# Moving the second half's key norm from a free-running thread to written places in the first half's chunk recursion

## The chip, the cores and the metric

The kernel runs on one core of one Trainium2 chip. The metric is the device time of one execution in microseconds (us); smaller is better. Five engines work side by side, each through its own list of instructions: TensorE (PE in the profile; its weight loads are shown apart as PEld), VectorE (DVE), ScalarE (ACT), GpSimd (POOL) and SyncE (SP, which here issues the weight transfers). An instruction that needs another engine's result waits for a semaphore, and what stands behind it in the same list waits with it.

## What is computed

The reference is one layer of a hybrid encoder for 256 tokens of width 2048: two attention branches, one RWKV-7 branch, a gated mix, and an MLP. The change touches only the RWKV-7 branch, 16 heads of 64 channels. Cut to what matters:

```python
kk_raw = k * k_k
r_h, k_h, v_h, a_h, kk = map(per_head, (r, k, v, a, kk_raw))
kk = kk / jnp.maximum(jnp.sqrt(jnp.sum(kk * kk, axis=-1, keepdims=True)), 1e-12)   # the key norm
decay = jnp.exp(-jnp.exp(per_head(w_log)))

def frame(state, inp):
    r_t, w_t, k_t, v_t, kk_t, kka_t = inp
    sa = jnp.einsum('bhvk,bhk->bhv', state, kk_t)
    state = state * w_t[:, :, None, :] - sa[..., None] * kka_t[:, :, None, :] + v_t[..., None] * k_t[:, :, None, :]
    return state, jnp.einsum('bhvk,bhk->bhv', state, r_t)
```

The state is carried over 256 tokens; afterwards every head is normalised (the gate norm of the kernel) and multiplied by a gate.

## The kernel before, in words

**The background work.** Nearly all of the time is a stream of weight blocks of 128x1024 floats. Each is loaded by SP into `raw` (3 buffers), split into a high part `whi` by ACT (L152) and a low part `wlo` by DVE (L153), and multiplied on PE in full 128x512 float matmuls (`gemm`, L168 to L176, and `tok`, L198 and L214).

**The foreground work.** The attention branches and the RWKV branch are Python generators ("threads"). The written program advances a modelled clock by 0.227 us for each large matmul (`tick`); whenever the clock passes a thread's due time the thread emits its next piece, so its small matmuls are written in between the large ones. `yield 2.0` means "come back 2 us later", `yield "kn1"` means "come back once that is marked".

**Who sets the order.** PE's list stands exactly as it is written (`tc.manual_schedule` for PE). The lists of ACT and DVE are arranged by a list scheduler at build time, except for instructions wrapped in `pin` (`tc.keep_in_program_order`), which stay in the order in which they are written. DVE, ACT and PE meet through tiles; a tile of a tag with one buffer can be written again only after the last reader of the one before.

**The RWKV branch.** The 16 heads are done as two halves of four channel tiles (`rwkv_half(0)`, `rwkv_half(1)`). Each half needs its key norm first (`key_norm`): ACT squares four tiles (L635), splits them (L646 on ACT, L647 on DVE), PE sums them per head with the matrix `bones` (L653), DVE clamps the sums (L655), ACT takes Ln and Exp (L659, L662) for a first inverse root, and DVE refines it by a Newton step (L667 to L672). The result is used in `rwkv_half` at L739.

A half ends in a recursion over four chunks of 64 tokens (`for c in range(4)`, L865 on). I call the chunks c0 to c3. In each chunk:

- PE multiplies the state into `xy` (L869, not in c0), ACT and DVE copy it to `rh` (L873, L874);
- PE solves the chunk (L882, mixed with L842, the part of the next chunk that is known already);
- the result goes from PSUM to `XT` in four copies: ACT, DVE for the first half of the heads (L886, L887), then ACT, DVE for the second half. I call them A0, V0, A1, V1;
- PE takes `XT` for the new state and the output (L894, L898, L903), DVE updates the state `PB` (L912 to L915), ACT copies the output (L917).

Between these steps PE works on the background stream. After c3 the half starts `gate_norm`, whose first steps are two groups of squares and splits on ACT and DVE (L944, L947, L948) and four summing matmuls on PE (L954). In the kernel before, the second half's key norm is started as a thread of its own in c0 of the first half (L905, L906), and its pieces come when their due times do. Its tiles: `b` (its squares and inverse roots), `sqh` (high and low part, in the one buffer of the tag `Ti`), `sq` (clamped sums).

Of the kernel before, what the change touches and what calls it, by code (L numbers as in the profile page):

```python
# [10 lines left out]
F32 = mybir.dt.float32  # L11
F32R = mybir.dt.float32r
AF = mybir.ActivationFunctionType
ALU = mybir.AluOpType
# [3 lines left out]
T = 256  # L18
# [32 lines left out]
def hybrid_block(ctx, tc, xt, x, gains, params, consts, lora, gup, wst, out):  # L51
    nc = tc.nc
    V, A, G, PE = nc.vector, nc.scalar, nc.gpsimd, nc.tensor
# [11 lines left out]
    def nm(s):  # L65
        uid[0] += 1
        return f"{s}_{uid[0]}"
# [4 lines left out]
    def mps():  # L72
        return pm.tile([128, 512], F32, tag="mps", name=nm("mps"), bufs=4)
# [25 lines left out]
    def mark(key, value=True):  # L99
        done[key], at[key] = value, clock[0]  # L100

    def start(gen):

        threads.append({"gen": gen, "need": None, "due": clock[0]})
# [146 lines left out]
    rp = p1.enter_context(tc.tile_pool(name="rp", bufs=1))  # L251
# [152 lines left out]
    for h in range(8):  # L404
        ps = qb[h] if h < 3 else unit(upk)
# [187 lines left out]
    bones = rp.tile([128, 128], F32R, name="bones")  # L593
# [34 lines left out]

    def key_norm(hf):
        PR = range(4 * hf, 4 * hf + 4)  # L630
        B6 = rp.tile([128, 6, T], F32, tag="b6", name=nm("b6"), bufs=1)
        rin = [B6[:, i, :] for i in range(4)]
        for i, p in enumerate(PR):
            yield f"k{p}"
            A.activation(rin[i], done[f"k{p}"], AF.Square, scale=P("kk", p))  # L635
        sq = []
        for both in ((0, 1),) if hf == 0 else ((0,), (1,)):
            sqh = []
            for i2 in both:
                s = B6[:, 2 * i2:2 * i2 + 2, :]  # L640
                if hf == 0:
                    hl = [rp.tile([128, 2, T], F32R, tag="BK", name=nm("sqh"), bufs=8) for _ in range(2)]
                else:
                    t = rp.tile([128, 4, T], F32R, tag="Ti", name=nm("sqh"), bufs=1)
                    hl = [t[:, 0:2], t[:, 2:4]]
                A.activation(hl[0], s, AF.Copy)  # L646
                V.tensor_tensor(hl[1], s, hl[0].bitcast(F32), ALU.subtract)  # L647
                sqh.append(hl)
            yield 3.8
            for hl in sqh:  # L650
                ps = mps()
                for n, part in enumerate(hl):
                    PE.matmul(ps.rearrange("p (a b) -> p a b", a=2), bones, part, start=n == 0, stop=n == 1)  # L653
                sq.append(rp.tile([128, 2, T], F32, tag="At", name=nm("sq"), bufs=2))
                V.tensor_scalar(sq[-1], ps.rearrange("p (a b) -> p a b", a=2), 1e-24, None, ALU.max)  # L655
        if hf:
            yield 2.0
        for i2 in range(2):
            A.activation(B6[:, 2 * i2:2 * i2 + 2, :], sq[i2], AF.Ln, scale=float(2.0 ** 20))  # L659
        for i2 in range(2):  # L660
            ri = B6[:, 2 * i2:2 * i2 + 2, :]
            A.activation(ri, ri, AF.Exp, scale=-0.5)  # L662
        yield 4.5
        sc = B6[:, 4:6, :]
        for i2 in range(2):
            ri = B6[:, 2 * i2:2 * i2 + 2, :]
            V.tensor_scalar(ri, ri, 1024.0, None, ALU.mult)  # L667
            V.tensor_tensor(sc, ri, ri, ALU.mult)
            yield 2.0
            V.tensor_tensor(sc, sc, sq[i2], ALU.mult)  # L670
            V.tensor_scalar(sc, sc, -0.5, 1.5, ALU.mult, ALU.add)
            V.tensor_tensor(ri, ri, sc, ALU.mult)  # L672
            yield 3.0
        kin[hf] = rin
        mark(f"kn{hf}")

    def rwkv_half(hf):
        PR = range(4 * hf, 4 * hf + 4)
        xw, xa, wl = done["low"]
        kn, lor = {}, {}  # L680
        kx = {p: done[f"k{p}"] for p in PR} if hf else {}

        def lora_load(p):
            if p in PR:
                lor[p] = rp.tile([128, 2, 128], F32, tag="zx", name=nm("lor"), bufs=1)
# [4 lines left out]
        def lora_split(p):  # L690
            if p in PR:
                raw = lor[p]
# [3 lines left out]

        lora_load(PR[0])
        if hf:
# [10 lines left out]
        rin = kin[hf]  # L709
        SC = rp.tile([128, 32, 128], F32, tag="SC", name=nm("SC"), bufs=1)  # L710
        At, Bt, Kt, bon = {}, {}, {}, {}
        ecol = rp.tile([128, 4, 4], F32, tag="ecol", name=nm("ecol"), bufs=2)
        for i, p in enumerate(PR):
            ps = mps()
# [6 lines left out]
            c = rp.tile([128, T], F32, tag="kkr", name=nm("cs"), bufs=1)  # L721
# [67 lines left out]
        for i2 in range(2):  # L789
            for cc in range(4):  # L790
                for h, hc in enumerate(HC):
                    for i, p in enumerate(PR[2 * i2:2 * i2 + 2]):
                        PE.matmul(pss[h][HC[i], i2 * 256 + cc * 64:i2 * 256 + cc * 64 + 64],
                                  done[f"v{p}"][hc, cc * 64:cc * 64 + 64], C("cen", hc, 64 * h, 64 * h + 64),
                                  start=i2 == cc == 0, stop=i2 == 1 and cc == 3)
# [9 lines left out]
        Ti = rp.tile([64, 32, 32], F32, tag="Ti", name=nm("Ti"), bufs=1)  # L805
# [8 lines left out]
        for s in range(31):  # L814
            n, m = 31 - s, s + 1
# [14 lines left out]
        ps = mps()  # L830
# [18 lines left out]
        ps = mps()  # L849
# [12 lines left out]
        def duo(ps, hc, d):  # L862
            return ps[hc, 128 * d:128 * d + 128].rearrange("p (a b) -> p a b", a=2)

        for c in range(4):  # L865
            if c:
                for i, p in enumerate(PR):
                    for h, hc in enumerate(HC):
                        PE.matmul(xy[h][HC[i % 2 ^ h], 64 * (i // 2):64 * (i // 2) + 64], Bt[p][hc, c, 0:64],  # L869
                                  PB[hc, i, hc], start=False, stop=i >= 2)  # L870
            rhs = rp.tile([64, 2, 2, 2, 64], F32, tag="rh", name=nm("rh"), bufs=1)
            for g, hg in enumerate(HC):
                A.activation(rhs[:, 0, g], xy[0][hg, 0:128].rearrange("p (a b) -> p a b", a=2), AF.Copy)  # L873
                V.tensor_copy(rhs[:, 1, g], xy[1][hg, 0:128].rearrange("p (a b) -> p a b", a=2))  # L874
            yield 2.0
            more = known(c + 1) if c < 3 else iter([None] * 9)
            if c < 3:
                first = next(more)
            ps = mps()
            for i in range(4):  # L880
                for h, hc in enumerate(HC):
                    PE.matmul(ps[hc, 64 * i:64 * i + 64], SC[0:64, i * 8 + h * 4 + c, 0:64],  # L882
                              rhs[:, h, i % 2 ^ h, i // 2], start=i == 0, stop=i == 3)
                    xy = next(more)
            for d in range(2):
                A.activation(XT[d][0:64, :, c, HC[0]], duo(ps, HC[0], d), AF.Copy)  # L886
                V.tensor_copy(XT[d][0:64, :, c, HC[1]], duo(ps, HC[1], d))  # L887
            yield 2.2
            ps = mps()
            psp, psy = ps[:, 0:256], ps[:, 256:512]  # L890
            if c < 3:
                for i, p in enumerate(PR):
                    for h, hc in enumerate(HC):
                        PE.matmul(psp[hc, 64 * i:64 * i + 64], Kt[p][:, c, hc], XT[i // 2][:, i % 2, c, hc],  # L894
                                  start=i == 0, stop=i == 3)
            for i, p in enumerate(PR):
                for h, hc in enumerate(HC):
                    PE.matmul(psy[hc, 64 * i:64 * i + 64], XT[i // 2][:, i % 2, c, hc], SC[:, i * 8 + h * 4 + c, 64:128],  # L898
                              start=i == 0, stop=c == 0 and i == 3)
            if c:  # L900
                for i, p in enumerate(PR):
                    for h, hc in enumerate(HC):
                        PE.matmul(psy[hc, 64 * i:64 * i + 64], PB[:, i, hc], Bt[p][:, c, 64:128], start=False,  # L903
                                  stop=i == 3)
            if c == 0 and hf == 0:  # L905
                start(key_norm(1))  # L906
            if c < 3:
                for h, hc in enumerate(HC):
                    s, e = PB[hc, :, hc], ecol[hc, :, c:c + 1].to_broadcast([64, 4, 64])
                    q = psp[hc].rearrange("p (a b) -> p a b", a=4)  # L910
                    if c:
                        V.tensor_tensor(s, q, s, ALU.add)  # L912
                        V.tensor_tensor(s, s, e, ALU.mult)
                    else:
                        V.tensor_tensor(s, q, e, ALU.mult)  # L915
            for i, p in enumerate(PR):
                A.activation(y[p][:, c * 64:c * 64 + 64], psy[:, 64 * i:64 * i + 64], AF.Copy)  # L917
            yield 2.6
        start(gate_norm(hf, y, bon))

    def gate_norm(hf, y, bon):
# [105 lines left out]
    for s in ("q", "k"):  # L1027
        lst = []
        for h in range(4):
            ps = unit(upk)  # L1030
            t = g1()
# [11 lines left out]
    for hf in range(2):  # L1043
        for s, mo in (("k", MU_K), ("r", MU_R), ("v", MU_V)):
            for p in range(4 * hf, 4 * hf + 4):
                ps = unit(upk)
# [176 lines left out]
    work, urgent, tasks, hl = [], [], [], {}  # L1223
# [256 lines left out]
    for b in range(4):  # L1480
        for sb in range(2):
            for d, F in enumerate(down(b, sb)):
# [199 lines left out]
```

## Time and profile before

| | us |
|---|---|
| median of 3 runs | 1505.39 |
| the runs | 1505.01, 1505.39, 1508.8 |
| the profiled execution, own time | 1504.03 |
| its span, first to last instruction | 1502.3 |
| outside the span (1504.03 - 1502.3) | 1.73 |
| PE, DVE, ACT busy in the span | 1482.0, 1215.5, 938.5 |
| mean granted TensorE clock | 0.995 |

The rows of the timeline give start, duration, engine, line, operation, output and inputs with their shapes, count, and in brackets the idle time of the engine before the row, with the engine, tile and line that ended it. Several instructions in a row that are alike are merged; durations in such a row overlap, because a new instruction starts before the one before has drained. For this reason I take costs on PE from start to start. First-half chunks lie at about 393 to 445 us of the span, second-half chunks at about 605 to 650 us.

### The profile page before, as it was taken

How to read it: one execution, taken by the hardware profiler on the slowest of the kernel's cores; microseconds unless marked ns; L12 is line 12 of the kernel's file. 1: busy time of each engine (PE TensorE's matmuls, PEld its weight loads, DVE VectorE, ACT ScalarE, POOL GpSimd, SP SyncE). 2: the span in 40 equal slices, each digit the busy share in tenths (PEclk: the TensorE clock that was granted, in tenths of full speed). 3: DMA queues.
4: the chain of work that ended last, by engine and by line, in shares of the span. 5: the costliest groups of instructions: out<-in, count | busy, mean ns of one | idle time of the engine just before them, and what ended most of it. 6: DMA issues, size and time to landing. Idle time of an engine off the chain costs nothing.

```text
span 1502.3 us, 22802 instructions
## 1 busy us (share of the span) xinstructions
PE 1482.0 (99%) x8401; PEld 1249.1 (83%) x8401; DVE 1215.5 (81%) x1687; ACT 938.5 (62%) x1398; POOL 91.3 (6%) x160
## 2 busy tenths in 40 slices
PE   9999999999999999999999999999999999999997
PEld 7888888888778888788887888888888888888885
DVE  7666677999769898567646788999899999899986
ACT  7465666664667554575444767777667676677662
POOL 0021000100001100000000000000000000000000
PEclk9999999999999999999999999999999999999998
DMA  7545545545535455445774668888888888888874
GB/s 258 196 150 188 174 169 170 178 164 193 187 116 181 160 181 199 153 147 197 264 281 169 223 207 241 266 241 246 259 263 251 264 255 228 252 259 272 257 247 152
DMA packets 107615, 317.70 MB, mean 211 GB/s; under 512 B 10736, under 2 KB 14704, under 8 KB 107248
## 3 DMA queue, kind: packets, MB, share of 16 engines
q1 hardware_dynamic: 94832, 284.91, 54.9%
q0 software_dynamic: 8064, 29.36, 10.4%
q10 hardware_dynamic: 4608, 1.97, 0.5%
q8 instruction: 66, 1.08, 0.3%
q14 instruction: 45, 0.37, 0.1%
HBM read 282.65 MB, written 4.19 MB: 191 GB/s over the span
## 4 chain that ended last, share of the span: by engine, by line
PE 69%; DVE 1%; issue 1%; POOL 0%; POOLq 0%; ACT 0%; DVEq 0%; ACTq 0%
PE gps L214 20%; PE gps L168 15%; PE gps L172 8%; PE gps L198 5%; PE mps L1412 3%; PE mps L1413 3%; PE mps L1414 3%; PE gps L1414 3%; PE gps L1412 2%; PE gps L1413 2%; PE gps L176 1%; PE mps L767 0%; PE mps L976 0%; DVE wlo L153 0%; PE mps L1103 0%
## 5 line engine op out<-in xcount | busy, mean ns | idle before, releaser
L153 DVE TENSOR_TENSOR wlo<-raw,whi 128x1024 fp32r<-128x1024 f32 x501 | 608.3, 1223 | 162.7 <-ACT whi L152 147.8
L152 ACT ACTIVATE whi<-raw 128x1024 fp32r<-128x1024 f32 x501 | 527.7, 1057 | 260.3 <-PE gps L214 94.1
L168 PE MATMUL gps<-pk,whi 128*128 128x512 f32 x1366 | 346.4, 393 | 0.6 <-ACT whi L152 0.4
L168 PEld LDWEIGHTS gps<-pk,whi 128*128 128x128 f32 x1366 | 253.0, 189 | 50.5 <-ACT whi L152 0.6
L214 PE MATMUL gps<-whi,pk 128*128 128x512 f32 x1144 | 288.5, 392 | 0.0
L214 PEld LDWEIGHTS gps<-whi,pk 128*128 128x128 f32 x1144 | 212.8, 188 | 44.3
L172 PEld LDWEIGHTS gps<-pk,wlo 128*128 128x128 f32 x1456 | 198.5, 190 | 14.4 <-DVE wlo L153 0.5
L172 PE MATMUL gps<-pk,wlo 128*128 128x256 f32 x1456 | 204.1, 282 | 0.0
L214 PE MATMUL gps<-wlo,pk 128*128 128x512 f32 x572 | 156.4, 392 | 0.0
L214 PEld LDWEIGHTS gps<-wlo,pk 128*128 128x128 f32 x572 | 106.3, 188 | 22.4 <-DVE wlo L153 0.3
L1304 ACT ACTIVATE sp<-gps 128x512 f32<-128x512 f32 x52 | 31.1, 598 | 86.2 <-PE gps L176 86.0
L1278 DVE TENSOR_TENSOR sp<-raw,sp 128x1024 fp32r<-128x1024 f32 x67 | 82.0, 1224 | 3.4 <-ACT sp L1277 3.1
L1277 ACT ACTIVATE sp<-raw 128x1024 fp32r<-128x1024 f32 x67 | 70.6, 1054 | 12.8 <-PE mps L1413 4.9
L198 PE MATMUL gps<-whi,pk 128*128 128x512 f32 x264 | 71.0, 391 | 0.0
L1412 PE MATMUL mps<-whi,fm 128*128 128x512 f32 x168 | 66.2, 394 | 0.0
L1413 PE MATMUL mps<-whi,fm 128*128 128x512 f32 x168 | 65.8, 392 | 0.0
L1414 PE MATMUL mps<-wlo,fm 128*128 128x512 f32 x168 | 65.5, 390 | 0.0
L1374 POOL DMA_DIRECT2D raw<-raw x40 | 35.0, 874 | 427.6 <-DVE wlo L153 106.0
L198 PEld LDWEIGHTS gps<-whi,pk 128*128 128x128 f32 x264 | 49.2, 188 | 10.4 <-ACT whi L152 0.2
L1414 PE MATMUL gps<-wlo,fm 128*128 128x512 f32 x126 | 49.2, 391 | 0.5 <-DVE wlo L153 0.5
L1371 DVE TENSOR_TENSOR raw<-raw,raw 128x1024 f32<-128x1024 f32 x40 | 48.9, 1223 | 0.4
L1412 PE MATMUL gps<-whi,fm 128*128 128x512 f32 x126 | 49.2, 391 | 0.0
(378 smaller groups left out, 1962.3 us busy)
## 6 DMA issues: line engine op xcount, KB each, us to landing
raw<-in_wst_dram SPq DMA_DIRECT2D x499, 512.0 KB, 4.3
raw<-raw POOLq DMA_DIRECT2D x40, 512.0 KB, 6.4
sp<-in_wst_dram SPq DMA_DIRECT2D x16, 512.0 KB, 5.3
raw<-sp POOLq DMA_DIRECT2D x8, 512.0 KB, 6.1
sp<-raw POOLq DMA_DIRECT2D x8, 512.0 KB, 6.6
x<-in_x_dram SPq DMA_DIRECT2D x8, 256.0 KB, 5.9
xs<-x SPq DMA_DIRECT2D x2, 1024.0 KB, 3.9
x<-xs SPq DMA_DIRECT2D x4, 512.0 KB, 6.0
```

The lines of the kernel that those rows point to most:

```text
L152: A.activation(hi, raw, AF.Copy)
L153: V.tensor_tensor(lo, raw, hi.bitcast(F32), ALU.subtract)
L168: PE.matmul(ps, hi[:, i * 128:i * 128 + 128], pks[i], start=first and i == 0, stop=False)
L172: PE.matmul(ps[:, 0:T], lo[:, i * 128:i * 128 + 128], pks[i][:, 0:T], start=False, stop=False)
L198: PE.matmul(ps[tt], pks[k][:, c:c + 128], w[:, (k - k0) * 512:(k - k0) * 512 + 512], start=k == 0 and part == 0 and w is hl[0], stop=w is ...
L214: PE.matmul(ps[tt], pks[k][:, c:c + 128], w[:, (k - k0) * 512:(k - k0) * 512 + 512], start=k == 0 and part == 0 and w is hl[0], stop=False)
L1277: A.activation(hi, raw, AF.Copy)
L1278: V.tensor_tensor(lo, raw, hi.bitcast(F32), ALU.subtract)
L1371: V.tensor_tensor(x, x, z, ALU.add)
L1412: PE.matmul(Q[f], p, w, start=d == 0 and i == 0, stop=False)
L1413: PE.matmul(Q[f], pl, w, start=False, stop=False)
L1414: PE.matmul(Q[f], p, wl, start=False, stop=d == nd - 1 and i == 1)
```

## The change

`key_norm(1)` no longer runs as a thread. `rwkv_half(0)` makes it a plain iterator, `beside`, and takes its next piece by `next(beside, None)` at written places: at the end of c0, then in each later chunk once behind the four `XT` copies and once at the chunk's end. So piece 1 (squares, first split) comes at the end of c0; the first sum and the second split behind the copies of c1; the second sum at the end of c1; Ln behind the copies of c2; Exp at the end of c2; the two Newton steps behind the copies and at the end of c3. All of its ACT and DVE instructions (not the clamp of the sums) are pinned to the written order. Ln of both halves of the data now stand together, and so do both Exp. The arithmetic is the same, and so is all of the first half's key norm.

```diff
     def key_norm(hf):
         PR = range(4 * hf, 4 * hf + 4)
+        keep = pin if hf else lambda ins: ins
...
+        def high_low(i2):
...
+            keep(A.activation(hl[0], s, AF.Copy))
+            keep(V.tensor_tensor(hl[1], s, hl[0].bitcast(F32), ALU.subtract))
+            return hl
+
+        def summed(hl):
+            ps = mps()
+            for n, part in enumerate(hl):
+                PE.matmul(ps.rearrange("p (a b) -> p a b", a=2), bones, part, start=n == 0, stop=n == 1)
+            sq.append(rp.tile([128, 2, T], F32, tag="At", name=nm("sq"), bufs=2))
+            V.tensor_scalar(sq[-1], ps.rearrange("p (a b) -> p a b", a=2), 1e-24, None, ALU.max)
+
         for i, p in enumerate(PR):
-            yield f"k{p}"
-            A.activation(rin[i], done[f"k{p}"], AF.Square, scale=P("kk", p))
...
+            if hf == 0:
+                yield f"k{p}"
+            keep(A.activation(rin[i], done[f"k{p}"], AF.Square, scale=P("kk", p)))
...
+        else:
+            hl = high_low(0)
+            yield
+            summed(hl)
+            hl = high_low(1)
+            yield
+            summed(hl)
+            yield
+        for i2 in range(2):
+            keep(A.activation(B6[:, 2 * i2:2 * i2 + 2, :], sq[i2], AF.Ln, scale=float(2.0 ** 20)))
         if hf:
-            yield 2.0
-        for i2 in range(2):
-            A.activation(B6[:, 2 * i2:2 * i2 + 2, :], sq[i2], AF.Ln, scale=float(2.0 ** 20))
+            yield
...
@@ rwkv_half
+        beside = iter(()) if hf else key_norm(1)
         for c in range(4):
...
                 V.tensor_copy(XT[d][0:64, :, c, HC[1]], duo(ps, HC[1], d))
+            if c:
+                next(beside, None)
             yield 2.2
...
-            if c == 0 and hf == 0:
-                start(key_norm(1))
...
                 A.activation(y[p][:, c * 64:c * 64 + 64], psy[:, 64 * i:64 * i + 64], AF.Copy)
+            next(beside, None)
             yield 2.6
+        for _ in beside:
+            pass
```

The same statement has another line number in the changed file. The pairs used below, before and after: L635 and L657 (square), L646 and L643 (high), L647 and L644 (low), L653 and L650 (sum), L655 and L652 (clamp), L659 and L672 (Ln), L662 and L677 (Exp), L667 to L672 and L682 to L688 (Newton), L873 and L890 (`rh`), L882 and L899, L886 and L903 (ACT's `XT` copies), L887 and L904 (DVE's), L894 and L913, L917 and L934, L947 and L967, L948 and L968, L954 and L974. L152 and L153 stay.

**First place: ACT in c1.** Here `whi` is the background split, `sqh` the second high part of the key norm, `b` its Ln and Exp, `XT` the copies A0 and A1. Before:

```order
L152 ACTIVATE whi_4301<-raw_4299 128x1024
L646 ACTIVATE sqh_4217<-b_773_4166 128x512
L659 ACT_TABLE_LOAD
L659 ACTIVATE b_773_4166<-sq_4215 128x512
L886 ACTIVATE XT_3445<-mps_4236 64x2x64
L662 ACT_TABLE_LOAD
L662 ACTIVATE b_773_4166<-b_773_4166 128x512
L886 ACTIVATE XT_3446<-mps_4236 64x2x64
```

In the changed kernel the same stretch, from the end of c0 on:

```order
L657 ACTIVATE b_773_4166<-g_496_2723,par 128x256
L643 ACTIVATE sqh_4171<-b_773_4166 128x512
L890 ACTIVATE rh_4200<-mps_4098 64x128 x2
L152 ACTIVATE whi_4219<-raw_4217 128x1024
L152 ACTIVATE whi_4306<-raw_4304 128x1024
L903 ACTIVATE XT_3445<-mps_4228 64x2x64
L903 ACTIVATE XT_3446<-mps_4228 64x2x64
L643 ACTIVATE sqh_4253<-b_773_4166 128x512
```

The two table loads, the Ln and the Exp have left c1, and A0 and A1 stand side by side; the four squares (the last of them is shown) and the first high part have come in ahead of `rh` from further up the list.

**Second place: ACT from the copies of c2 to `rh` of c3.** `g` is the chunk's output copy. Before (the loads and Ln, Exp of the second data half stand further up, ahead of the copies of c2):

```order
L886 ACTIVATE XT_3445<-mps_4357 64x2x64
L886 ACTIVATE XT_3446<-mps_4357 64x2x64
L152 ACTIVATE whi_4469<-raw_4467 128x1024
L917 ACTIVATE g_754_4073<-mps_4394 128x64
...
L917 ACTIVATE g_757_4076<-mps_4394 128x64
L152 ACTIVATE whi_4502<-raw_4500 128x1024
L873 ACTIVATE rh_4455<-mps_4354 64x128 x2
```

After:

```order
L903 ACTIVATE XT_3446<-mps_4353 64x2x64
L672 ACT_TABLE_LOAD
L672 ACTIVATE b_773_4166<-sq_4251 128x512
L672 ACTIVATE b_773_4166<-sq_4302 128x512
L152 ACTIVATE whi_4464<-raw_4462 128x1024
...
L934 ACTIVATE g_757_4076<-mps_4392 128x64
L677 ACT_TABLE_LOAD
L677 ACTIVATE b_773_4166<-b_773_4166 128x512 x2
L152 ACTIVATE whi_4500<-raw_4498 128x1024
L890 ACTIVATE rh_4453<-mps_4350 64x128 x2
```

One load with two Ln has moved in behind A1 of c2, one load with two Exp in front of the `whi` and `rh` of c3. Over the whole program ACT has two table loads less.

**Third place: DVE from V1 of c3 into the gate norm.** `gn` is the gate norm's low part, `gup` the split of a gate weight. Before:

```order
L887 COPY XT_3446<-mps_4479 64x2x64
L153 TENSOR_TENSOR wlo_4585<-raw_4582,whi_4584 128x1024
L948 TENSOR_TENSOR gn_4556<-gn_4557,gn_4555 128x512
L937 TENSOR_TENSOR gup_4645<-gup_4562,gup_4645 128x128
L938 TENSOR_TENSOR gup_4645<-gup_4562,gup_4645 32x128
L948 TENSOR_TENSOR gn_4556<-gn_4557,gn_4555 128x512
```

After:

```order
L904 COPY XT_3446<-mps_4474 64x2x64
L682 TENSOR_SCALAR b_773_4166<-b_773_4166 128x512
L683 TENSOR_TENSOR b_773_4166<-b_773_4166 128x512
L686 TENSOR_TENSOR b_773_4166<-b_773_4166,sq_4251 128x512
...
L968 TENSOR_TENSOR gn_4556<-gn_4557,gn_4555 128x512
L686 TENSOR_TENSOR b_773_4166<-b_773_4166,sq_4302 128x512
L153 TENSOR_TENSOR wlo_4585<-raw_4582,whi_4584 128x1024
L687 TENSOR_SCALAR b_773_4166<-b_773_4166 128x512
L957 TENSOR_TENSOR gup_4645<-gup_4562,gup_4645 128x128
L688 TENSOR_TENSOR b_773_4166<-b_773_4166 128x512
L958 TENSOR_TENSOR gup_4645<-gup_4562,gup_4645 32x128
L968 TENSOR_TENSOR gn_4556<-gn_4557,gn_4555 128x512
```

Nine of the ten Newton instructions, which stood between the chunks c1 and c2 before, have come in here, six ahead of the first low part, one between it and `wlo`, two between `wlo` and the second low part; the tenth (L682) stands just ahead of V0 of c3.

PE's list changes in two places only: the first sum's pair of matmuls moves from in front of L882 of c1 to right behind it, and the second sum's pair moves two pairs of matmuls up, to right behind L903 of c1. The lists of POOL and SP are the same in both kernels.

More of the change, by code (lines that the diff above doesn't have):

```diff
@@ L630, in key_norm @@
         PR = range(4 * hf, 4 * hf + 4)
+        keep = pin if hf else lambda ins: ins
         B6 = rp.tile([128, 6, T], F32, tag="b6", name=nm("b6"), bufs=1)
         rin = [B6[:, i, :] for i in range(4)]
-        for i, p in enumerate(PR):
-            yield f"k{p}"
[L635 to L648, printed above, removed]
-            yield 3.8
[L650 to L655, printed above, removed]
@@ new lines, in key_norm @@
+        sq = []
+        def high_low(i2):
+            s = B6[:, 2 * i2:2 * i2 + 2, :]
+            if hf == 0:
+                hl = [rp.tile([128, 2, T], F32R, tag="BK", name=nm("sqh"), bufs=8) for _ in range(2)]
+            else:
+                t = rp.tile([128, 4, T], F32R, tag="Ti", name=nm("sqh"), bufs=1)
+                hl = [t[:, 0:2], t[:, 2:4]]
+            keep(A.activation(hl[0], s, AF.Copy))
+            keep(V.tensor_tensor(hl[1], s, hl[0].bitcast(F32), ALU.subtract))
+            return hl
@@ new lines, in summed @@
+        def summed(hl):
[4 more added lines that the diff above has]
+            V.tensor_scalar(sq[-1], ps.rearrange("p (a b) -> p a b", a=2), 1e-24, None, ALU.max)
+        for i, p in enumerate(PR):
+            if hf == 0:
+                yield f"k{p}"
+            keep(A.activation(rin[i], done[f"k{p}"], AF.Square, scale=P("kk", p)))
@@ L656, in key_norm @@
+        if hf == 0:
+            hl = [high_low(i2) for i2 in range(2)]
+            yield 3.8
+            for x2 in hl:
+                summed(x2)
+        else:
+            hl = high_low(0)
[7 more added lines that the diff above has]
+            keep(A.activation(B6[:, 2 * i2:2 * i2 + 2, :], sq[i2], AF.Ln, scale=float(2.0 ** 20)))
         if hf:
-            yield 2.0
-        for i2 in range(2):
-            A.activation(B6[:, 2 * i2:2 * i2 + 2, :], sq[i2], AF.Ln, scale=float(2.0 ** 20))
+            yield
@@ L660, in key_norm @@
         for i2 in range(2):
             ri = B6[:, 2 * i2:2 * i2 + 2, :]
-            A.activation(ri, ri, AF.Exp, scale=-0.5)
+            keep(A.activation(ri, ri, AF.Exp, scale=-0.5))
         yield 4.5
@@ L666, in key_norm @@
             ri = B6[:, 2 * i2:2 * i2 + 2, :]
[L667 to L672, printed above, removed]
+            keep(V.tensor_scalar(ri, ri, 1024.0, None, ALU.mult))
+            keep(V.tensor_tensor(sc, ri, ri, ALU.mult))
+            if hf == 0:
+                yield 2.0
+            keep(V.tensor_tensor(sc, sc, sq[i2], ALU.mult))
+            keep(V.tensor_scalar(sc, sc, -0.5, 1.5, ALU.mult, ALU.add))
+            keep(V.tensor_tensor(ri, ri, sc, ALU.mult))
             yield 3.0
```

## Prediction

> **What bounds the kernel now.** I read the page's head first.
>
> ```profile
> span 1502.3 us, 22802 instructions
> PE 1482.0 (99%) x8401; PEld 1249.1 (83%) x8401; DVE 1215.5 (81%) x1687; ACT 938.5 (62%) x1398; POOL 91.3 (6%) x160
> ```
>
> PE is the bound: 1502.3 - 1482.0 = 20.3 us of the span is idle there, and nothing that ACT or DVE save counts unless PE stops waiting. So I asked next for PE's waits in the stretch of the edit, 385 to 450 us.
>
> ```profile
> PE mps L894 <- DVE XT L887: 1.6, 3, 1.0
> PE mps L894 <- ACT XT L886: 1.2, 1, 1.2
> PE mps L898 <- DVE XT L887: 0.3, 1, 0.3
> ```
>
> That is all: 3.1 us, and every wait is for the `XT` copies of a chunk. The timeline of PE places them: c1 at 415, c2 at 428, c3 at 441. The last two rows are c1 of the second half, where no key norm runs beside.
>
> ```profile
> 414.93 0.45 PE L894 MATMUL mps<-XT,Kt 128*64 128x64 f32 x8
> 416.56 0.33 PE L894 MATMUL mps<-XT,Kt 128*64 128x64 f32 x2 [1.18 <-ACT XT L886]
> 418.38 1.20 PE L214 MATMUL gps<-whi,pk 128*128 128x512 f32 x4
> ...
> 427.84 0.33 PE L894 MATMUL mps<-XT,Kt 128*64 128x64 f32 x2
> 430.25 0.39 PE L894 MATMUL mps<-XT,Kt 128*64 128x64 f32 x5 [1.05 <-DVE XT L887]
> 431.56 1.20 PE L214 MATMUL gps<-wlo,pk 128*128 128x512 f32 x4
> ...
> 440.51 0.56 PE L898 MATMUL mps<-SC,XT 128*64 128x64 f32 x10
> 442.20 1.20 PE L214 MATMUL gps<-whi,pk 128*128 128x512 f32 x4
> ...
> 625.80 0.69 PE L894 MATMUL mps<-XT,Kt 128*64 128x64 f32 x16
> 627.35 1.19 PE L214 MATMUL gps<-whi,pk 128*128 128x512 f32 x4
> ```
>
> From start to start the block takes 627.35 - 625.80 = 1.55 us where nothing interferes; in c1 it takes 418.38 - 414.93 = 3.45, in c2 431.56 - 427.84 = 3.72. So the stalls cost 1.90 and 2.17, more than the bracketed gaps, because a stalled pipeline must also fill again.
>
> What makes the copies late? ACT and then DVE in c1, and one DVE row of c2:
>
> ```profile
> 411.56 0.61 ACT L646 ACTIVATE sqh<-b 128x512 fp32r<-128x512 f32 x1
> 412.19 1.28 ACT L659 ACT_TABLE_LOAD   x1
> 413.48 0.63 ACT L659 ACTIVATE b<-sq 128x512 f32<-128x512 f32 x1
> 414.14 0.27 ACT L886 ACTIVATE XT<-mps 64x128 f32<-64x128 f32 x1
> 414.43 1.28 ACT L662 ACT_TABLE_LOAD   x1
> 415.72 0.63 ACT L662 ACTIVATE b<-b 128x512 f32<-128x512 f32 x1
> 416.26 0.25 ACT L886 ACTIVATE XT<-mps 64x128 f32<-64x128 f32 x1
> ...
> 416.73 0.28 DVE L887 COPY XT<-mps 64x128 f32<-64x128 f32 x1
> 429.90 0.29 DVE L887 COPY XT<-mps 64x128 f32<-64x128 f32 x1
> ```
>
> The copies go A0, V0, A1, V1. In c1 a table load with its Ln stands ahead of A0, another with its Exp between A0 and A1: A1 ends at 416.51 and PE resumes at 416.56. In c2 the Newton steps hold V0 and V1 back on DVE; V1 ends at 430.19, PE resumes at 430.25. The key norm causes both stalls, by where its pieces stand in the queues.
>
> **The change part by part.**
>
> *What is taken away.* By the order, nothing of Ln, Exp or Newton is left in c1, and in c2 nothing of them is left ahead of the copies. If the copies then come in time, 1.90 + 2.17 = 4.07 us of PE go. The two table loads that vanish (2 x 1.28 of ACT) are part of this, not more: ACT is no bound by itself. The matmuls are the same in number; the two moved pairs of sums cost PE the same elsewhere.
>
> *Do the copies of c1 come in time?* New in front of them: on ACT four squares and a split ahead of `rh`, then two `whi` of which one stood earlier; on DVE the low parts, a `wlo` and the clamp of the first sum (now between V0 and V1). Rows for the walk:
>
> ```profile
> 397.76 1.69 ACT L635 ACTIVATE b<-g,par 128x256 f32<-128x256 f32 x4
> 406.59 0.57 ACT L917 ACTIVATE g<-mps 128x64 f32<-128x64 f32 x4 [1.80 <-DVE PB L915]
> 407.03 1.08 ACT L152 ACTIVATE whi<-raw 128x1024 fp32r<-128x1024 f32 x1
> 408.96 0.56 ACT L873 ACTIVATE rh<-mps 64x128 f32<-64x128 f32 x2 [0.85 <-PE mps L869]
> ...
> 410.02 0.69 DVE L1075 SCALAR_TENSOR_TENSOR m<-th,gps 128x512 f32<-128x512 f32 x1
> 412.81 1.22 DVE L153 TENSOR_TENSOR wlo<-raw,whi 128x1024 fp32r<-128x1024 f32 x1
> ```
>
> ACT is free at 407.16 after the output copies. With whole durations, nothing overlapping: squares 1.69, high part 0.61, `rh` 0.56, `whi` 1.08 gives 411.10 for the first `whi`. DVE then: `wlo` 1.22, `m` 0.69, `wlo` 1.22, V0 0.28, clamp 0.69 (an instruction of `m`'s size), V1 0.28: 415.48. ACT's second `whi` ends at 412.18 and is no hindrance. These rows start some 0.07 us before the one ahead has ended (407.03 against 407.16), so with seven such overlaps V1 ends at about 415.0. PE reaches the block at 414.93, as before, since the pair of sums only changes its place ahead of that; V1's data are wanted by the ninth of 16 matmuls, about 0.25 later, at 415.2. So V1 comes between 0.2 early and 0.3 late. I take 0.1 late: c1 gives 1.8, between 1.6 and 1.9.
>
> *The sums.* The first pair now stands behind L899 and needs the first low part (DVE, about 410.2 by the same walk), over 1 us early. The second stands behind the block of c1, at about 416.5 (414.93 + 1.55), and needs high part (after A1, 415.1 to 415.4) and low part (after V1, 415.7 to 416.2, by 0.69): on time by at least 0.3. No cost; if V1 of c1 came later than I think, PE would wait here for the same delay, not for more.
>
> *The copies of c2.* In front of A0 only a `whi`, between V0 and V1 one `wlo`, as in before; what stood there besides, 0.43 + 3 x 0.69 us of Newton steps, is gone. These four took 2.50 us; without them DVE ends V1 at 430.19 - 2.50 = 427.69 in the old time base, and PE reaches the block at 427.84 and wants V1's data about 0.25 later: the whole 2.17 is gained.
>
> *Exp ahead of c3's `rh`.* This is the new wait that the change could create: on ACT one table load, two Exp and one `whi` now stand between the output copies of c2 and `rh`.
>
> ```profile
> 432.63 0.57 ACT L917 ACTIVATE g<-mps 128x64 f32<-128x64 f32 x4 [2.87 <-DVE PB L912]
> ...
> 437.40 0.68 PE L882 MATMUL mps<-rh,SC 64*64 64x64 f32 x16
> ```
>
> PE leaves the block of c2 at 431.56 and wants `rh` 5.84 us later. The copies begin 1.07 after that; 1.07 + 0.57 + 1.28 + 2 x 0.63 + 1.08 + 0.56 = 5.82 with whole durations, about 5.4 with the overlaps. It fits by 0 to 0.4 us: no cost, but it is the thinnest cover of the change, and if it is gone PE waits one for one.
>
> [...]
>
> *Newton steps behind c3.* Nine instructions now stand on DVE between V1 of c3 and the gate norm's second low part.
>
> ```profile
> 441.02 0.29 DVE L887 COPY XT<-mps 64x128 f32<-64x128 f32 x1
> 444.54 1.23 DVE L153 TENSOR_TENSOR wlo<-raw,whi 128x1024 fp32r<-128x1024 f32 x1 [3.23 <-ACT whi L152]
> 448.33 0.69 DVE L948 TENSOR_TENSOR gn<-gn,gn 128x512 fp32r<-128x512 f32 x1 [1.47 <-ACT gn L947]
> 422.04 0.43 DVE L671 TENSOR_SCALAR b<-b 128x512 f32<-128x512 f32 x1
> ...
> 449.39 1.10 PE L954 MATMUL mps<-gn,bones 128*128 128x512 f32 x4
> ```
>
> They cost 3 x 0.43 + 6 x 0.69 = 5.43 us against 3.23 + 1.47 = 4.70 of idle time. Walked through from 441.31: six steps to 444.9, low part 0.69, step 0.69, `wlo` 1.23, step 0.43, `gup` about 0.3, step 0.69, `gup` 0.3, low part 0.69: 449.9 to 450.1. It is wanted by the fourth matmul of L954, about 450.1: 0 to 0.1 us of wait. `wlo` here ends near 447.6 and is read only after L954. The results themselves are read in the second half, far behind. The stall of c3, 0.3 by the waits, stays: A1 and V1 there still stand behind `whi` and `wlo`.
>
> *Sum.* 1.8 + 2.17, less 0 to 0.1: 4.0 us, between 3.6 and 4.1. The profiled execution took 1504.03 and would take 1500.0. It is 1.36 below the median of the runs; carried to the median, 1505.39 - 4.0 = 1501.4, -0.27%.
>
> **The rivals.**
>
> *c1 gains nothing* (1503.2). If ACT's and DVE's full queues in c1 bring V1 1.9 us or more later than walked, PE stalls there as before and only c2's 2.17 remains. For it: both queues are full from 407 to 415. Against: walked with whole durations V1 is only 0.3 late. Chance 0.17, partial cases included.
>
> *The Exp load costs double* (1502.2). If ACT stays shut behind the Exp load of c2 for as long again as the load lasts, `rh` comes at 5.4 + 1.28 = 6.68 against 5.84, and PE waits 0.84 in c3: 1505.39 - 4.0 + 0.84. The rows at 412.19 and 414.43 show the next instruction 1.29 after each load's start, which speaks against it. Chance 0.04. [...]
>
> *The gain is given back* (1505.4). The change removes the stalls but PE waits as much elsewhere, for instance on weights behind a later `whi` of c1. Against: those `whi` are read 6 us and more after they are made. Chance 0.09.
>
> *Slower: the backlog on DVE* (1505.8). If none of the nine Newton steps fits into the 3.23 us gap behind c3, because Exp is not ready when V1 ends, all 5.43 us come ahead of the second low part: it ends at 449.02 + 5.43 = 454.45 against 450.1, PE waits 4.35 in L954, and 1505.39 - 3.97 + 4.35 = 1505.8; each further us adds one. It decides as soon as Exp ends later than 441.3 in the old time base. Walked, Exp ends 1.07 + 0.57 + 1.28 + 1.26 = 4.2 after 431.56, at 435.7, so 5 us would have to be lost first. Chance 0.05.
>
> *c3 gains too* (1500.8). Its block takes 442.20 - 440.51 = 1.69, with no L894; if the shift cured its wait, some 0.6 more would go. Nothing in the order says so. Chance 0.08.
>
> **How the numbers follow.** The forecast has 0.57. About 0.3%, 4.5 us, is what a measurement of this kernel can tell from no change, and 4.0 lies just inside. Same: most of the forecast, since 4.0 turns to over 4.5 only by scatter (the three runs span 3.8 us), and nearly all of the smaller gains: 0.71. Faster: about a quarter of the forecast, most of the c3 case: 0.24. Slower by over 0.3% needs the backlog and more, or scatter on no gain: 0.05. The range goes from the profiled execution less 4.5, 1499.5, to the backlog's neighbourhood, 1505.6, which takes in every case but the worst.
>
> **What would show it right or wrong.** In the changed profile PE's waits at L913 in c1 and c2 should be gone or below 0.3 us, the block of c2 should take about 1.55 and that of c1 up to 1.8; c3 keeps about 0.3; L899 of c3, L650 and L974 should show no wait over 0.1. ACT should have one Ln and one Exp load between c2's copies and c3's `rh`. Wrong would be: a wait of L899 for `rh` (the table load), of L974 for `gn` (the backlog), of L650 for `sqh`, or a stall in c1 of about 1.9; or the stalls gone and the time unchanged.

## The result and the profile after

Ten runs of the changed kernel have a median of 1500.34 us (1497.93 to 1504.09), ten of the kernel before 1504.46 (1502.23 to 1508.8). The ratio is 0.9971, with an interval of 0.9962 to 0.9981: 4.1 us less, -0.29%, which was forecast as -4.0. Single runs of either kernel lie 6 to 7 us apart at the ends, so I judge each kernel below by a stretch of the first half's recursion, where nothing but the edit differs, and the change itself by the medians.

The profiled execution of the changed kernel is the slowest of its ten, 1504.09 us. The head of its page:

```profile
span 1502.3 us, 22797 instructions
PE 1483.2 (99%) x8401; PEld 1249.9 (83%) x8401; DVE 1216.3 (81%) x1687; ACT 934.9 (62%) x1396; POOL 91.1 (6%) x160
```

By its span the change would have done nothing. The stretch says otherwise. PE's waits from 385 to 450 us, all of them:

```profile
PE mps L917 <- DVE XT L904: 0.3, 1, 0.3
```

And PE's timeline there, with the start of each chunk's block and of what follows it, up to the gate norm's sums:

```profile
404.34 0.69 PE L913 MATMUL mps<-XT,Kt 128*64 128x64 f32 x16
...
413.84 1.07 PE L214 MATMUL gps<-wlo,pk 128*128 128x512 f32 x4
415.04 0.69 PE L913 MATMUL mps<-XT,Kt 128*64 128x64 f32 x16
...
416.59 0.73 PE L650 MATMUL mps<-sqh,bones 128*128 128x512 f32 x2
...
425.99 0.69 PE L913 MATMUL mps<-XT,Kt 128*64 128x64 f32 x16
...
427.53 1.19 PE L214 MATMUL gps<-wlo,pk 128*128 128x512 f32 x4
...
433.37 0.68 PE L899 MATMUL mps<-rh,SC 64*64 64x64 f32 x16
...
434.55 1.09 PE L214 MATMUL gps<-wlo,pk 128*128 128x512 f32 x4
...
436.47 0.56 PE L917 MATMUL mps<-SC,XT 128*64 128x64 f32 x10
...
438.16 1.19 PE L214 MATMUL gps<-whi,pk 128*128 128x512 f32 x4
...
445.34 0.86 PE L974 MATMUL mps<-gn,bones 128*128 128x512 f32 x3
```

The block of c1 takes 416.59 - 415.04 = 1.55, that of c2 427.53 - 425.99 = 1.54: both stalls are gone, and c3 keeps its 1.69. The same reading of every kernel of this study gives the table; "stretch" is its row's sum, from the start of c0's block to the start of the gate norm's sums.

| us from start to start | c0 to c1 | c1 block | to c2 | c2 block | to c3 | c3 block | to sums | stretch |
|---|---|---|---|---|---|---|---|---|
| before | 10.50 | 3.45 | 9.46 | 3.72 | 8.95 | 1.69 | 7.19 | 44.96 |
| after | 10.70 | 1.55 | 9.40 | 1.54 | 8.94 | 1.69 | 7.18 | 41.00 |
| e1, after again | 10.68 | 1.55 | 9.42 | 1.55 | 8.94 | 1.69 | 7.16 | 40.99 |
| e2, four loads | 10.67 | 1.55 | 9.43 | 1.55 | 12.15 | 1.08 | 7.18 | 43.61 |
| e3, places alone | 10.47 | 1.55 | 9.61 | 3.70 | 8.96 | 1.69 | 7.18 | 43.16 |
| e4, pins alone | 10.55 | 3.19 | 9.64 | 1.84 | 8.94 | 1.69 | 7.17 | 43.02 |
| e5, no second key norm | 10.03 | 1.55 | 8.95 | 1.55 | 8.93 | 1.70 | 7.18 | 39.89 |
| e6, copies on ACT | 10.48 | 1.54 | 9.43 | 1.55 | 8.94 | 1.08 | 7.16 | 40.18 |

So the stretch gains 44.96 - 41.00 = 3.96, and the two executions of the changed kernel agree on it to 0.01. In the one profiled first the gain holds until a late transfer near 1391 us. ACT's row for it:

```profile
1390.95 1.06 ACT L152 ACTIVATE whi<-raw 128x1024 fp32r<-128x1024 f32 x1 [4.28 <-DMA raw<-raw]
```

PE's timeline behind it, with two gaps:

```profile
1397.33 0.50 PE L1434 MATMUL gps<-wlo,fm 128*128 128x512 f32 x1 [0.99 <-DVE wlo L153]
...
1399.49 3.55 PE L168 MATMUL gps<-pk,whi 128*128 128x512 f32 x8 [0.96 <-DVE junk L1439]
1402.88 1.11 PE L172 MATMUL gps<-pk,wlo 128*128 128x256 f32 x8
```

PE waits 0.99 + 0.96 us, and the eight matmuls then take 1402.88 - 1399.49 = 3.39 from start to start, with the clock granted at 0.50 from 1399.3 to 1402.7. That is over 850 us behind the last instruction that reads the key norm's results (L755, at 516.9); whether it belongs to the change is what the first experiment asks.

### The profile page after: what moved, and what is told of

Same layout as the page of the kernel before. It is cut to its first block, busy times and chain, and to the rows that moved or that the text cites. A ratio compares the mean times of both kernels' runs of the same rounds, so it can differ in the third digit from the quotient of the medians.

```text
span 1502.3 us, 22797 instructions
## 1 busy us (share of the span) xinstructions
PE 1483.2 (99%) x8401; PEld 1249.9 (83%) x8401; DVE 1216.3 (81%) x1687; ACT 934.9 (62%) x1396; POOL 91.1 (6%) x160
## 3 DMA queue, kind: packets, MB, share of 16 engines
q8 instruction: 66, 1.08, 0.3%
## 4 chain that ended last, share of the span: by engine, by line
PE 95%; DVE 2%; DMA 1%; issue 1%; ACT 1%; POOL 1%; SPq 0%; POOLq 0%; DVEq 0%; ACTq 0%
PE gps L214 28%; PE gps L168 23%; PE gps L172 13%; PE gps L198 7%; PE mps L1432 3%; PE mps L1433 3%; PE mps L1434 3%; PE gps L1434 2%; PE gps L1432 2%; PE gps L1433 2%; PE gps L176 2%; DMA raw<-in_wst_dram 1%; PE gps L328 1%; DVE wlo L153 1%; PE mps L783 1%
## 5 line engine op out<-in xcount | busy, mean ns | idle before, releaser
L153 DVE TENSOR_TENSOR wlo<-raw,whi 128x1024 fp32r<-128x1024 f32 x501 | 607.8, 1221 | 165.1 <-ACT whi L152 150.4
L152 ACT ACTIVATE whi<-raw 128x1024 fp32r<-128x1024 f32 x501 | 527.4, 1056 | 264.4 <-PE gps L214 92.4
```

Source lines behind the costliest of these rows:

```text
L152: A.activation(hi, raw, AF.Copy)
L153: V.tensor_tensor(lo, raw, hi.bitcast(F32), ALU.subtract)
```

## The experiments

My theory is that the whole gain is the two stalls, and that they are a matter of place: whatever stands ahead of or between A0, V0, A1 and V1 in the two queues. The rivals are that the two table loads saved are the gain, that it is lost again later, and that one half of the change (the places, or the pins) does it alone. e2 to e5 have one time each, which decides nothing beside the scatter; their profiles do.

**e1: the changed kernel once more.** No edit.

> The changed kernel once more. Question: in the profiled execution of the changed kernel PE runs 4.0 us ahead of before from 428 us on, but from 1391 to 1402 us it loses 4.2 us, and the span is 1502.3 as before. Theory (that execution's own mishap: late transfers and a half-clock window there): the profile shows the blocks of c1 and c2 at 1.5 to 1.6 us each again, c3 at 1.69, PE's stretch from L913 of c0 to L974 at 41.0 (before: 44.96), and no loss of 4 us near 1395; its span is below that of before unless another half-clock window falls into it. Rival (the change causes the late loss): the loss near 1395 is there again, about 4 us. Time: 3 to 5 us below before by the theory, as in the result; by the rival the profiled execution equals before again.

Ten runs: 1500.85 us (1497.68 to 1502.61) against 1505.11 in 14 runs of before, ratio 0.997, interval 0.996 to 0.9979. The profiled execution took 1498.42. Near 1395 us its timeline of PE has no gap:

```profile
1395.12 0.40 PE L1434 MATMUL gps<-wlo,fm 128*128 128x512 f32 x1
1395.35 1.98 PE L168 MATMUL gps<-pk,whi 128*128 128x512 f32 x8
1397.17 1.12 PE L172 MATMUL gps<-pk,wlo 128*128 128x256 f32 x8
```

The same eight matmuls take 1397.17 - 1395.35 = 1.82. The late loss belongs to that one execution and not to the change; nothing is given back.

**e2: four table loads again, at the new places.**

```diff
-        for i2 in range(2):
-            keep(A.activation(B6[:, 2 * i2:2 * i2 + 2, :], sq[i2], AF.Ln, scale=float(2.0 ** 20)))
-        if hf:
-            yield
-        for i2 in range(2):
-            ri = B6[:, 2 * i2:2 * i2 + 2, :]
-            keep(A.activation(ri, ri, AF.Exp, scale=-0.5))
+        for group in ((0,), (1,)) if hf else ((0, 1),):
+            for i2 in group:
+                keep(A.activation(B6[:, 2 * i2:2 * i2 + 2, :], sq[i2], AF.Ln, scale=float(2.0 ** 20)))
+            for i2 in group:
+                ri = B6[:, 2 * i2:2 * i2 + 2, :]
+                keep(A.activation(ri, ri, AF.Exp, scale=-0.5))
+            if hf and group == (0,):
+                yield
```

> The changed kernel with Ln and Exp grouped by data half again: load, Ln, load, Exp of the first data half behind the copies of c2, the same of the second at the end of c2, so four table loads as in before, but none ahead of a copy. Theory (a stall comes only where the pieces stand ahead of what PE waits for): blocks of c1 and c2 stay at 1.55, but rh of c3 comes 1.4 to 2.1 later than in the changed kernel (one load and Ln more in front, and the output copies later), it is 0.3 early there, so PE waits 1.1 to 1.8 at L899 of c3, for ACT's rh; stretch c0 to the gate norm's sums 42.1 to 42.8. Rival (the two table loads saved on ACT are the gain): stalls at the copies of c1 or c2 come back, together near 2.6. [...]

One time, 1503.74. c1 and c2 stay clean (1.55 each), so the saved loads are not what the gain is made of. But the second pair now stands ahead of c3's `rh`. ACT, from c2's output copies on:

```profile
428.36 0.55 ACT L935 ACTIVATE g<-mps 128x64 f32<-128x64 f32 x4
428.92 1.28 ACT L673 ACT_TABLE_LOAD   x1
...
430.86 1.28 ACT L676 ACT_TABLE_LOAD   x1
...
432.69 1.04 ACT L152 ACTIVATE whi<-raw 128x1024 fp32r<-128x1024 f32 x1
433.63 0.55 ACT L891 ACTIVATE rh<-mps 64x128 f32<-64x128 f32 x2
```

PE in the same place:

```profile
433.94 0.86 PE L900 MATMUL mps<-rh,SC 64*64 64x64 f32 x16 [1.44 <-ACT rh L891]
...
435.30 1.82 PE L214 MATMUL gps<-wlo,pk 128*128 128x512 f32 x4
...
438.76 0.69 PE L918 MATMUL mps<-SC,XT 128*64 128x64 f32 x16
```

The windows view of e2 right behind it (time, then busy time of PE, weight loads, DVE, ACT and POOL, the granted clock, DMA share and GB/s):

```profile
435.40:438.80 3.40, 3.40 (x11) 2.17 (x9) 2.22 (x6) 1.25 (x3) 0.20 (x1) 0.50 0.55 186
```

The thin cover at `rh` is real: with two loads more on ACT it turns into a wait of 1.44, as expected. The stretch, 43.61, is longer than expected and than that wait makes it, since for 3.4 us behind it PE is granted half its clock: eight matmuls take 438.76 - 435.30 = 3.46, against 436.47 - 434.55 = 1.92 in the changed kernel. These 1.54 and the 1.44, less the 0.61 of c3's own stall, which the delay hides, make 2.37 of the 2.61 by which e2's stretch exceeds the changed kernel's.

**e3: the places without the pins.** The thread is replaced by the written places, but the scheduler may move ACT's and DVE's pieces.

```diff
-        keep = pin if hf else lambda ins: ins
+        keep = lambda ins: ins
```

> The changed kernel with nothing pinned: the pieces are written at the new places, but the scheduler may move them forward again. In its order four table loads stand in c1 and c2: Ln and Exp of the first data half behind A1 of c1, of the second around rh of c2, the first Newton steps of both in front of V0 of c2. Theory (queue places decide): c1 is clean, block 1.55 to 1.8, since both copies stand ahead of the loads; in c2 V0 and V1 come 2 us late behind the Newton steps on DVE, block 3.5 to 4.0 as before; stretch c0 to L974 about 43.2. Rival (the written places are the gain, pins a detail): both blocks near 1.55, stretch 41.0. Rival (pins are all of it): both blocks as in before, stretch 45.

One time, 1503.05; c1 is cured, c2 is as bad as before (3.70). DVE in c2:

```profile
425.12 0.43 DVE L687 TENSOR_SCALAR b<-b 128x512 f32<-128x512 f32 x1
425.58 0.69 DVE L688 TENSOR_TENSOR b<-b 128x512 f32<-128x512 f32 x1
426.19 0.29 DVE L904 COPY XT<-mps 64x128 f32<-64x128 f32 x1
```

Written behind the copies, the Newton steps are put ahead of them by the scheduler: V0 starts at 426.19, while PE reached the block at 425.48. They are late because they wait in turn for ACT, whose table loads stand ahead of A0 (425.00) here as in before.

**e4: the pins without the places.** The kernel before, its thread kept, with the second half's key norm pinned; the squares, Ln, Exp and the Newton steps are wrapped in the same way as the two lines shown.

```diff
+        keep = pin if hf else lambda ins: ins
...
-                A.activation(hl[0], s, AF.Copy)
-                V.tensor_tensor(hl[1], s, hl[0].bitcast(F32), ALU.subtract)
+                keep(A.activation(hl[0], s, AF.Copy))
+                keep(V.tensor_tensor(hl[1], s, hl[0].bitcast(F32), ALU.subtract))
...
```

> The kernel before, its thread and its places, with the instructions of the second half's key norm pinned as in the changed kernel. By its order Ln and Exp stand behind A1 of c1 (two loads in all) and the Newton steps behind the copies of c2, but a high part stands ahead of A0 of c1 and a whi that waits for PE, with its wlo, between A0 and A1 and ahead of V1. Theory (queue places decide): c1 still stalls, V1 ends near 416.7, block 3.0 to 3.5; c2 is clean, block 1.55; c3 1.69; stretch c0 to L954 42.5 to 43. Rival (the written places are the gain): both blocks as before, stretch 45. Rival (pins and the batched loads are all): both blocks 1.55, stretch 41.

One time, 1502.85. Now c2 is nearly clean (1.84) and c1 stalls (3.19), for another reason than in before. DVE in c1:

```profile
413.17 0.29 DVE L888 COPY XT<-mps 64x128 f32<-64x128 f32 x1
413.39 2.35 DVE L153 TENSOR_TENSOR wlo<-raw,whi 128x1024 fp32r<-128x1024 f32 x2
415.65 0.29 DVE L888 COPY XT<-mps 64x128 f32<-64x128 f32 x1
```

Two `wlo` have slipped between V0 and V1. c2 was expected at 1.55; the 0.29 more come with a V1 that starts only at 427.13, behind another `wlo`, while PE reached the block at 426.95. Places alone are worth 44.96 - 43.16 = 1.80, pins alone 44.96 - 43.02 = 1.94, both together 3.96: the places cure c1, the pins nearly cure c2.

**e5: no key norm in the second half.** GpSimd fills its four inverse roots with a constant instead, so the output is not the reference's. The ceiling for any place that the key norm could be given.

```diff
         sq = []
+        if hf:
+            G.memset(B6[:, 0:4, :], 2.5e-3)
+            yield
+            kin[hf] = rin
+            mark(f"kn{hf}")
+            return
```

> The changed kernel without the second half's key norm: GpSimd fills its four inverse roots with the constant 0.0025, so the second half's keys are scaled wrongly and the output is not the reference's. It is the floor for any placing of these pieces. Theory (the pieces now cost PE only their own four sums): blocks of c1, c2 and c3 as in the changed kernel, 1.55, 1.55, 1.69; stretch from L913 of c0 to the gate norm's sums shorter than 41.0 by the two pairs of matmuls alone, 0.9 to 1.2 us: 39.8 to 40.1. Rival (queues are still in PE's way, for instance the clamp or the Newton steps): 39.5 or less.

One time, 1501.47; the stretch is 39.89, 1.11 below the changed kernel's. Its four summing matmuls alone are 4 x 0.23 = 0.92, by the rate of 1.82 / 8 above. The other 0.19 is the late start of c1's block in the changed kernel, which is told below. PE's waits:

```profile
PE mps L923 <- DVE XT L910: 0.3, 1, 0.3
```

c3's stall is there without any key norm: it isn't the key norm's.

**e6: in the first half all four copies of `XT` on ACT.**

```diff
-                V.tensor_copy(XT[d][0:64, :, c, HC[1]], duo(ps, HC[1], d))
+                if hf == 0:
+                    A.activation(XT[d][0:64, :, c, HC[1]], duo(ps, HC[1], d), AF.Copy)
+                else:
+                    V.tensor_copy(XT[d][0:64, :, c, HC[1]], duo(ps, HC[1], d))
```

> The changed kernel with all four XT copies of a first-half chunk on ACT, in the order A0, V0's, A1, V1's, instead of turns between ACT and DVE; it is meant against the stall of c3, where A1 and V1 stand behind a whi that waits for PE and its wlo. Theory (the handing to and fro leaves gaps into which such rows are put; on one engine the four run back to back): c1 and c2 stay at 1.55, c3 falls from 1.69 to 1.1, since the copies end near 1.6 us after L899 starts, 1.5 before PE wants them; ACT has 4 copies more per chunk ahead of rh, but rh keeps its place; stretch 40.4 instead of 41.0, time 4 to 5 us below before (0.6 more than the changed kernel, within the scatter). Rival (ACT becomes late: with 0.5 us more in c2, rh of c3 loses its 0.3 us): PE waits 0.1 to 0.4 at L899 of c3 and the stretch stays at 40.8 to 41. Rival (c3's wait has another cause): c3 stays at 1.69.

Five runs: 1498.82 us (1497.97 to 1501.46) against 1505.51 in nine of before, ratio 0.9963, interval 0.9949 to 0.9976. ACT in c3:

```profile
432.50 0.27 ACT L903 ACTIVATE XT<-mps 64x128 f32<-64x128 f32 x1 [1.03 <-PE mps L899]
...
433.38 0.28 ACT L905 ACTIVATE XT<-mps 64x128 f32<-64x128 f32 x1
```

PE where c1 and c3 begin:

```profile
412.42 1.07 PE L214 MATMUL gps<-wlo,pk 128*128 128x512 f32 x4
413.42 0.69 PE L916 MATMUL mps<-XT,Kt 128*64 128x64 f32 x16
...
434.88 0.69 PE L920 MATMUL mps<-SC,XT 128*64 128x64 f32 x16
...
435.96 1.19 PE L214 MATMUL gps<-whi,pk 128*128 128x512 f32 x4
```

The four copies take 433.66 - 432.50 = 1.16 us with nothing between them, and PE has no wait left from 385 to 450. c3 gains 1.69 - 1.08 = 0.61, and c1 another 0.2 that I hadn't expected. Of the kernels tried that compute the whole layer it is the fastest; against the changed kernel the 0.82 of the stretch is shown, while the 1.5 between the medians lies within the intervals.

## Why the prediction came out right

- **PE is the bound and only its waits count: right.** ACT has 938.5 - 934.9 = 3.6 us less work, and e2, which has the loads back, still has c1 and c2 clean (1.55 each). That a stall costs more than its bracketed gap can be read in before: one matmul of the block takes 0.22 us from start to end, sixteen in a row 0.69, so each time the row is broken about 0.2 more is lost (an estimate from these two).
- **c1, 1.8 forecast: 1.70, but the missing 0.2 is not the one that was walked.** The block gains its 1.90, but it starts 415.04 - 413.84 = 1.20 after the four matmuls ahead of it, where e6 (412.42 to 413.42) has 1.00. DVE of the changed kernel in c1:

```profile
412.63 1.22 DVE L153 TENSOR_TENSOR wlo<-raw,whi 128x1024 fp32r<-128x1024 f32 x1
413.88 0.29 DVE L904 COPY XT<-mps 64x128 f32<-64x128 f32 x1
414.20 0.69 DVE L652 TENSOR_SCALAR sq<-mps 128x512 f32<-128x512 f32 x1
414.93 0.29 DVE L904 COPY XT<-mps 64x128 f32<-64x128 f32 x1
```

V1 came nearly as walked: it ends at 415.22, and a block that had started on time, at 414.84, would have wanted it 0.25 later, at 415.09. (The overlap that the walk took off per row, 0.07, is not what its rows show: 407.03 against 407.16 is 0.13.) But the block does not stop half way for V1; its first matmul, which does not read V1's data, is late already. What ends just before it is the clamp of the first sum, at 414.89, 0.15 ahead; it stands on DVE behind V0 and the `wlo` ahead of that. In e1 and e2 the block is as late (412.71 to 413.91 and 412.88 to 414.08, 1.20 each). The trace has a wait of PE's weight loader at L913 there, at 414.94, for a semaphore that DVE counts up, last at 414.91 with the clamp; in before the same wait is met at 412.21, well ahead of the block (414.93). In e6 the clamp ends at 413.02, 0.40 before the block, and the block starts on time, as it does in e5, which has no sums (412.58 to 413.58, 1.00), and in e3 (413.33 to 414.32, 0.99). The likely reason stands in the kernel: the tag `mps` has four PSUM buffers, two hold `xy` of the next chunk, one the solution that V1 still reads, so the block has to write where the clamp has just read. That is argued, since no run changes the number of buffers. So the step "No cost" for the moved sums was wrong by some 0.2: in before, the first sum and its clamp were done ahead of L882. Without the clamp V1 would have cost 415.22 - 415.09 = 0.13 by an estimate from the same rows, so the forecast was close partly by luck. The waits view shows nothing of it, because the whole block starts later instead.

- **c2, 2.17 forecast: 2.18, by a walk that was incomplete.** The Newton steps do hold the copies: in e3, with the steps back ahead of V0, the block takes 3.70 again. But the walk priced DVE alone. Before:

```profile
426.43 0.43 DVE L667 TENSOR_SCALAR b<-b 128x512 f32<-128x512 f32 x1 [1.61 <-ACT b L662]
427.37 0.27 ACT L886 ACTIVATE XT<-mps 64x128 f32<-64x128 f32 x1
430.11 0.68 DVE L672 TENSOR_TENSOR b<-b 128x512 f32<-128x512 f32 x1
```

Of the 2.50 us that it took off V1, L672 stands behind V1, and ahead of the first step DVE had been idle for 1.61 us until ACT's Exp came. The same loads on ACT held A0 too, which ends at 427.64. With the Newton steps alone gone, V0, a `wlo` and V1 (0.29 + 1.21 + 0.29) would still have ended near 429.4, by an estimate from these rows, 1.3 us after PE wants V1 (428.09). By this estimate both queues had to be cleared, as the change does, and the walked 427.69 hit by luck: in the changed kernel V1 ends at 425.69, 0.30 before the block starts, which is 427.54 in the old time base.

- **Exp ahead of c3's `rh`, forecast to fit by 0 to 0.4: 0.3.** ACT of the changed kernel:

```profile
429.21 1.28 ACT L677 ACT_TABLE_LOAD   x1
430.50 1.15 ACT L677 ACTIVATE b<-b 128x512 f32<-128x512 f32 x2
...
432.51 0.55 ACT L890 ACTIVATE rh<-mps 64x128 f32<-64x128 f32 x2
```

`rh` ends at 433.06 and PE takes it at 433.37. Exp starts 1.29 after its load's start, so the load cost its own 1.28 here and nothing behind it. That ACT stays shut for as long again, which the rival with the double price supposes, no run shows: in e2, too, the Ln and the Exp ahead of c3's `rh` start 1.29 after their loads' starts (428.92 to 430.21, 430.86 to 432.15), and two more loads cost a wait of 1.44.

- **Newton steps behind c3, forecast 0 to 0.1 of wait: none.** DVE's second low part:

```profile
444.90 0.69 DVE L968 TENSOR_TENSOR gn<-gn,gn 128x512 fp32r<-128x512 f32 x1
```

It ends at 445.59; the fourth matmul of L974, wanting it, comes at 445.34 + 3 x 0.23 = 446.03. The walk was 0.3 to 0.5 too long, because rows that follow each other overlap by more than I took off. The rival of the backlog needed Exp 5 us late; it was on time.

- **c3 keeps its 0.3: right,** and e5 and e6 show whose it is: not the key norm's, but that of `whi` and `wlo` (and two short splits of `gup`), which stand ahead of A1 and V1.
- **The sum.** The terms held in size: -1.90 + 0.20 - 2.18 = -3.88; the stretch measures -3.96, the medians -4.1 and in e1 -4.3. The forecast of 1501.4 is 1.1 above the median mostly because it started from the median of three runs, 1505.39, where ten gave 1504.46; 1504.46 - 4.0 is 1500.5. That the gain would lie near the 0.3% that can be told from no change was right: the interval, 0.19 to 0.38%, holds it.

What stays open: why the late transfer near 1391 us came in one execution and not in the other.

## What to carry to other kernels

Where PE waits for a chain of copies that alternates between two queues, look at what stands ahead of and between the links: here the key norm's rows there cost PE 1.90 us in c1 and 2.18 in c2, and a few rows further on the same ones left both blocks at 1.55 and 1.54. Look also at who still reads the PSUM buffer that PE writes next; here a clamp on a busy queue seems to have held PE for 0.2 us, which no wait on an operand shows. Writing side work at a place holds only if the scheduler may not move it, and pinning holds only if the place is good; here each alone cured about one chunk of two (1.80 and 1.94 of 3.96). The chain that changed engine at every link had side work of both queues between its links; on one engine, in c3 of e6, it took 1.16 us with nothing between.

## What the runs showed of the hardware

**Stretches of 3.4 us at half the clock followed waits of 1.44 to 1.95 us, in some executions and not in others.** Besides its start and its end, the profiled execution of before has one stretch in which PE is granted 0.50 of its clock (818.40 to 821.82), the first of the changed kernel has two (815.58 to 818.99 and 1399.26 to 1402.67), and e2 has the one from 435.40 to 438.80. One place shows that it is no property of the kernel alone. It lies far behind the edit, in code that all kernels share. The windows of before:

```profile
815.00:818.40 3.40, 1.53 (x10) 0.71 (x8) 3.34 (x9) 0.82 (x3) 0.54 (x1) 1.00 0.55 233
818.40:821.80 3.40, 3.24 (x10) 2.25 (x11) 3.37 (x9) 2.81 (x9) 0.00 (x0) 0.50 0.18 77
```

The same in e1:

```profile
809.90:813.30 3.40, 1.53 (x10) 0.70 (x8) 3.34 (x9) 0.76 (x3) 0.54 (x1) 1.00 0.55 231
813.30:816.70 3.40, 3.05 (x18) 2.33 (x19) 3.40 (x10) 3.00 (x9) 0.00 (x0) 1.00 0.18 77
```

Both are busy 1.53 of 3.4 us, with a wait of 1.87; in before the next 3.4 us run at 0.50, in e1 at 1.00. In e2 a single wait of 1.44 was followed by such a stretch, in the first profile of the changed kernel two of 0.99 and 0.96 together, while the 1.18 of c1 in before was not.

The traces of before and of the changed kernel say in part where such stretches fall. Within one run the changes of the granted clock lie whole multiples of 3.413 us apart: in before at 12.86, 818.40 and 821.82 (236 and 237 times 3.4133 behind the first), in the changed kernel at 13.45, 815.58, 818.99, 1399.26 and 1402.67 (235, 236, 406 and 407 times). Counted on each of these two runs' own grid, and away from start and end, PE was busy for 1.54 us (before), 2.01 and 1.69 us (changed) in the three steps at full clock that a halved one followed, and for 2.25 or more in all others. The wait of 1.18 in before lies in a step that is busy 2.30. The stretch of e1 shown above, busy 1.53 like that of before, is followed by one at full clock (813.30 to 816.70), though it was not counted on a grid of its own; so these few cases give no sharp limit.

In e2 such a stretch cost 1.54 us on top of the wait. They do not make most of the scatter of the runs: six of the first ten runs of the changed kernel have the same granted clock, 0.995, and their spans go from 1496.1 to 1500.8.
